# Two neighbouring rows of w_down on a partition: one layout of the expert weights against another

## The chip, the cores and the metric

The kernel runs on one core of a Trainium2 chip (trn2); the other cores are idle. The metric is the device time of one execution in microseconds, smaller is better; several executions give a median. Engine names are those of the profile: PE is TensorE (PEld its weight loads), DVE is VectorE, ACT ScalarE, POOL GpSimd, SP SyncE, whose queue issues nearly all DMAs. A line such as L188 is a line of the kernel before.

## The reference, cut to what matters

The program is one block of a streaming encoder on 256 frames of 1024 channels: a mixer (latent attention and a gated short convolution), then a mixture of 32 experts, of which each frame takes four. What the change touches is the second half:

```python
def expert_block(args):
    xb, e = args
    gu = xb @ w_gu[e] + b_gu[e]
    gate, up = gu[:, :D_EXPERT], gu[:, D_EXPERT:]
    gate = jnp.minimum(gate, SWIGLU_LIMIT)
    up = jnp.clip(up, -SWIGLU_LIMIT, SWIGLU_LIMIT)
    act = (up + 1.0) * (gate * jax.nn.sigmoid(gate * SWIGLU_ALPHA))
    return act @ w_down[e] + b_down[e]
```

All is float32. For one expert `w_gu[e]` is 1024 x 2048 (8 MB of 1024 x 1024 bytes each) and `w_down[e]` is 1024 x 1024 (4 MB). The sum over the 1024 channels of `act @ w_down[e]` may be taken in any order, so long as the activation's channel and the row of `w_down` that it multiplies belong together.

## The kernel before, in words

The mixer comes first (some 260 us), then a loop over the 32 experts. Each expert has at most 64 frames (`CAP`); more than that would be handled by `beyond()`, whose branch is not taken on these inputs.

**Weights.** The experts' weights stream through a ring of 22 slots of 8 KB a partition (`slot`, tag `wslot`). `todo` (L162 to L168) sets the order of the loads: the eight chunks of `w_gu` of expert e, then the four of `w_down` of expert e-1, and so on; the loads of a chunk are 1 MB each (`prefetch`, L171). A chunk of `w_gu` (L185) is 128 rows, one row of 8 KB on each partition. A chunk k of `w_down` (L188) is 256 rows; by the view `dn_v` (L159) partition p takes row 256k + p and row 256k + 128 + p, two pieces of 4 KB that lie 512 KB apart in memory. The last expert's `w_down` (L174 to L182) is loaded in another cut, first the columns 0 to 255 and 512 to 767, then the others, in pieces of 1 KB.

All these loads are issued by SP in the order of `todo`. The program hands out eight DMA semaphores in turn, so an issue waits until the DMA eight issues before it has landed; it also waits until the slot that it writes is free, which is PE's doing. The waits as the program has them, for the last whole expert but one on SP (DMAHW0 to DMAHW7 are the eight semaphores, PE the release of the slot):

```order
L188 DMA wslot<-in_w_down 128x2x1024 [waits DMAHW7_49,PE_49]
L188 DMA wslot<-in_w_down 128x2x1024 [waits DMAHW0_49,PE_49]
L188 DMA wslot<-in_w_down 128x2x1024 [waits DMAHW1_49,PE_49]
L188 DMA wslot<-in_w_down 128x2x1024 [waits DMAHW2_49,PE_49]
L185 DMA wslot<-in_w_gu 128x2048 [waits DMAHW3_49,PE_49]
L185 DMA wslot<-in_w_gu 128x2048 [waits DMAHW4_49,PE_49]
L185 DMA wslot<-in_w_gu 128x2048 [waits DMAHW5_49,PE_49]
L185 DMA wslot<-in_w_gu 128x2048 [waits DMAHW6_49,PE_49]
L185 DMA wslot<-in_w_gu 128x2048 [waits DMAHW7_49,PE_49]
L185 DMA wslot<-in_w_gu 128x2048 [waits DMAHW0_49,PE_49]
L185 DMA wslot<-in_w_gu 128x2048 [waits DMAHW1_49,PE_49]
L185 DMA wslot<-in_w_gu 128x2048 [waits DMAHW2_49,PE_49]
```

Counted back by eight in this cycle of twelve, the four `w_down` issues wait for the first four `w_gu` loads of the same cycle, the first four `w_gu` issues for the last four `w_gu` loads of the cycle before, and the last four `w_gu` issues for that cycle's `w_down`. The change leaves these waits as they are.

**Compute.** For an expert, `gate_up` multiplies its 64 gathered frames by the eight `w_gu` chunks into `pg` (L1014); the gate's half-columns 0 to 511 stand on PSUM partitions 0 to 63 and 512 to 1023 on 64 to 127. `act` (L1018) makes the activation `sgm`, 128 partitions by 512. `act_t` (L1028) turns it: four transposes on PE (L1031), each of 128 channels that are neighbours in `sgm`, and one copy by DVE to `aT` (L1033). `down` (L1043) takes the four `w_down` chunks, two row blocks a chunk, and multiplies each block with the columns of `aT` that hold its channels (`down_block`, L1040); DVE scales the result to `yp` (L1054). `scatter` (L1060) spreads two experts' `yp` to the 256 frames, in `acc`; every fourth expert `gather` (L982) picks the frames of the next four. The `down` of expert e-1 runs after the `gate_up` of expert e. For the last expert, e = 31, the `down` of e = 30 has the `act_t` of e = 31 in its middle (`late`), and then the last `down` goes in two column halves (L1220 ff.), each with its share of the scatter (L1242), of the squares (L1248) and of the output.

Of the kernel before, what the change touches and what calls it, by code (L numbers as in the profile page):

```python
# [16 lines left out]
P = 128  # L17
D = 1024
T = 256
NT = 2  # L20
NQ = 8
# [10 lines left out]
DE = 1024  # L32
# [19 lines left out]
def ap_of(a, offset, dims):  # L52
    return bass.AP(tensor=a.tensor, offset=a.offset + offset, ap=dims)
# [3 lines left out]
def block_kernel(ctx, tc, x, c, positions, w_ada, b_ada, norm_mix_g, w_in, q_norm_g, w_uq, kv_norm_g,  # L57
                 w_ukv, w_up_attn, conv_w, w_up_conv, w_o, norm_ffn_g, router_w, router_b, w_gu, b_gu,
                 w_down, b_down, norm_final_g, out, dbg=None):
    nc = tc.nc  # L60
    V, S, G, TE = nc.vector, nc.scalar, nc.gpsimd, nc.tensor
    load = nc.sync.dma_start
# [10 lines left out]
    def slot(shape, name="wslot", dtype=F32):  # L73
        t = slots.tile([P, 2048], dtype, name=name, tag="wslot")
        n = 1
        for s in shape:
            n *= s
        t = t[:, :n]
        if len(shape) == 2:
            t = t.rearrange("p (a b) -> p a b", b=shape[1])  # L80
        elif len(shape) == 3:
            t = t.rearrange("p (a b c) -> p a b c", b=shape[1], c=shape[2])
        return t
# [20 lines left out]
    ident = keep.tile([P, P], F32, name="ident")  # L104
# [51 lines left out]
            V.tensor_scalar(dst, ps, a_col[:, n, j:j + 1], sh_col[:, n, j:j + 1], op0=ALU.mult, op1=ALU.add)  # L156

    gu_v = w_gu.rearrange("o e (q p) f -> p (o e) q f", p=P)
    dn_v = w_down.rearrange("o e (k q p) d -> p (o e) k q d", q=2, p=P)  # L159


    todo = []  # L162
# [8 lines left out]
    def prefetch(n):  # L171
        while len(here) < n and todo:
            e, k = todo.pop(0)
            if e == NE - 1 and k >= NQ:  # L174

                w = slot([4, 2, 256])
                b = 4 * ((k - NQ) % 2)
                cols = ap_of(w_down, (e * DE + b * P) * D + 256 * ((k - NQ) // 2),
                             [[D, P], [P * D, 4], [512, 2], [1, 256]])
                for q in ([slice(0, 4)] if k % 2 == 0 else (slice(0, 2), slice(2, 4))):  # L180
                    for h in range(2):
                        load(w[:, q, h], cols[:, q, h])  # L182
            elif k < NQ:
                w = slot([2048])
                load(w, gu_v[:, e, k, :])  # L185
            else:
                w = slot([2, D])
                load(w, dn_v[:, e, k - NQ])  # L188
            here.append(w)

    with tc.tile_pool(name="front", bufs=1) as fr, \
            tc.tile_pool(name="tp", bufs=4, space=bass.MemoryType.PSUM) as tpp:

        def tpt():
            return tpp.tile([P, 512], F32, name="tp")
# [94 lines left out]
        for q2 in range(4):  # L290
            p = tpt().rearrange("p (q t) -> p q t", t=T)
# [103 lines left out]
        for half in range(2):  # L395
            for k in range(4):
                q = 4 * half + k
                S.activation(hT[0][:, q, :], xps[q // 2][:, q % 2, :], AF.Identity, bias=sh_col[:, 0, q:q + 1],
                             scale=a_col[:, 0, q:q + 1])
                q = 4 * half + (k + 2) % 4  # L400
# [329 lines left out]
        for h in range(2):  # L730
            p = tpt()
# [168 lines left out]
        p = tpt()  # L900
# [5 lines left out]
        p = tpt()  # L906
# [53 lines left out]
    def pmt():  # L960
        return pmi.tile([P, 512], F32, name="pm")
# [9 lines left out]
    def gather(rks, hs=None, oh=None):  # L971

        n = len(rks) * CAP
        c = slice(4 * CAP - n, 4 * CAP)
        oh = (onehot(rks) if oh is None else oh).rearrange("p i a b -> p i (a b)")
        hs = hs or hsel()
        for q2 in range(4):
            p = pmt()[:, :2 * n].rearrange("p (q c) -> p q c", c=n)
            for q in range(2):
                qs = slice((2 * q2 + q) * P, (2 * q2 + q + 1) * P)  # L980
                for i in range(NT):
                    TE.matmul(p[:, q, :], xs[:, i, qs], oh[:, i, :n], start=(i == 0), stop=(i == NT - 1))  # L982
            for q in range(2):
                affine(hs[q2 // 2][:, 2 * (q2 % 2) + q, c], p[:, q, :], 1, 2 * q2 + q, q2)
        return hs

    def placed(rks, ws):

        ow = mo.tile([P, NT, 2, CAP], F32, name="ow", bufs=1)
        for i in range(NT):  # L990
            for k in range(2):
                V.tensor_scalar(ow[:, i, k, :], iota2[:, 0, :], rks[k][:, i, :], ws[k][:, i, :],
                                op0=ALU.is_equal, op1=ALU.mult)
        return ow

    def spread(ow):

        p = pmt()
        for i in range(NT):
            TE.transpose(p[:, i * P:(i + 1) * P], ow[:, i].rearrange("p a b -> p (a b)"), ident)  # L1000
        s2 = mo.tile([P, T], F32, name="s2")
        S.activation(s2, p[:, :T], AF.Copy)  # L1002
        return s2
# [14 lines left out]
    def act(pg):  # L1018
        ga = mo.tile([P, 512], F32, name="ga", bufs=1)
        sgm = mo.tile([P, 512], F32, name="sgm")  # L1020
        V.tensor_scalar(ga, pg[:, 0, :], LIMIT, None, op0=ALU.min)  # L1021
        S.activation(sgm, ga, AF.Sigmoid, scale=ALPHA)  # L1022
        V.tensor_scalar(pg[:, 1, :], pg[:, 1, :], LIMIT, -LIMIT, op0=ALU.min, op1=ALU.max)
        V.tensor_mul(ga, ga, sgm)
        V.scalar_tensor_tensor(sgm, pg[:, 1, :], 1.0, ga, op0=ALU.add, op1=ALU.mult)
        return sgm

    def act_t(a):  # L1028
        p = pmt().rearrange("p (q c) -> p q c", c=P)
        for q in range(4):  # L1030
            TE.transpose(p[:, q, :], a[:, q * P:(q + 1) * P], ident)  # L1031
        aT = mo.tile([P, 4, P], F32, name="aT")
        V.tensor_copy(aT, p)  # L1033
        return aT
# [28 lines left out]
    def chunk(k):  # L1063
        prefetch(1)
        return here.pop(0)
# [8 lines left out]
    def beyond():  # L1074

        cur = keep.tile([P, 1], F32, name="cur")
        lane = keep.tile([P, NE], F32, name="lane")
        V.memset(cur, 0.0)
        G.iota(lane, pattern=[[1, NE]], base=0, channel_multiplier=0, allow_small_or_imprecise_dtypes=True)
        at = keep.tile([P, NE], F32, name="at")  # L1080
        pick = keep.tile([P, NE], F32, name="pick")
        we = keep.tile([P, NT, 1], F32, name="we")
        re = keep.tile([P, 5, NT, 1], F32, name="re")
        row = slot([2, 2, 512], "row")
        ring = [slot([2, D], "ring") for _ in range(4)]
        reg = nc.values_load(flag[0:1, 0:1], min_val=0, max_val=T)
        with tc.If(reg > CAP):
            with tc.For_i(0, NE, 1) as e:
                G.dma_start(row[0:1], b_gu[:, bass.ds(e, 1), :].rearrange("o a (n g f) -> (o a) n g f", n=2, f=512))
                gu_e = w_gu[:, bass.ds(e, 1)].rearrange("o a (q p) f -> p (o a q) f", p=P)  # L1090
                dn_e = w_down[:, bass.ds(e, 1)].rearrange("o a (k p) d -> p (o a k) d", p=P)

                def gu_in(q):
                    w = ring[q % 4].rearrange("p a b -> p (a b)")
                    G.dma_start(w, gu_e[:, q, :])
                    return w

                def dn_in(k):
                    G.dma_start(ring[k], dn_e[:, 2 * k:2 * k + 2, :])
                    return ring[k]  # L1100

                V.tensor_scalar(at, lane, cur, None, op0=ALU.is_equal)
                V.tensor_scalar(cur, cur, 1.0, None, op0=ALU.add)
                for i in range(NT):
                    V.scalar_tensor_tensor(pick, at, 1.0, rk[:, i, :], op0=ALU.mult, op1=ALU.mult,
                                           accum_out=re[:, 0, i, :])
                    V.scalar_tensor_tensor(pick, at, 1.0, wgt[:, i, :], op0=ALU.mult, op1=ALU.mult,
                                           accum_out=we[:, i, :])
                for b in range(1, 5):
                    V.tensor_scalar(re[:, b], re[:, 0], -float(b * CAP), None, op0=ALU.add)  # L1110
                rks = [re[:, b] for b in range(1, 5)]
                hb = gather(rks)

                def bias_row(n, o):
                    for g in range(2):
                        TE.matmul(o[64 * g:64 * g + 64, :], ones[0:1, :64], row[0:1, n, g, :], start=True,
                                  stop=False, skip_group_check=True)

                for b in range(3):
                    if b % 2 == 0:  # L1120
                        s2 = spread(placed(rks[b:b + 2], [we, we]))
                        yp = mo.tile([P, D], F32, name="yp", bufs=1)
                    a = act(gate_up(hb, CAP * b, bias_row, gu_in))
                    down(act_t(a), dn_in, yp, b % 2)
                    if b == 1:
                        scatter(s2, yp)
                scatter(s2, yp, CAP)
# [5 lines left out]
    for e in range(NE):  # L1133
# [24 lines left out]
        a = act(pg)  # L1158
# [33 lines left out]
        if e == 10:  # L1192
# [9 lines left out]
            p = pmt()  # L1202
# [4 lines left out]
            for h in range(2):  # L1207
                p = pmt()
# [6 lines left out]
        if e == 18:  # L1215
            gfin_b = mo.tile([P, D], F32, name="gfin_b", tag="gfin", bufs=1)
            G.dma_start(gfin_b[0:1, :], norm_final_g.rearrange("(o d) -> o d", o=1))
            for h in range(2):
                p = pmt()
# [7 lines left out]
    o = slot([NT, D], "o")  # L1227
    s2 = s2s.pop(NE // 2 - 1)
    aT = down(aT, chunk, yp, 0, a)
    for c in range(2):  # L1230
        cs = slice(256 * c, 256 * c + 256)
        py = pmt()[:, :256]
        for b in range(8):
            if b % 4 == 0:
                w = chunk(b)
# [56 lines left out]
```

## Time and profile before

| | us |
|---|---|
| median of 3 runs | 1198.37 (1194.8 to 1198.66) |
| the profiled execution | 1196.22 |
| its span, first to last instruction | 1194.5 |
| PE busy | 1075.9 |
| DVE busy | 387.0 |
| ACT busy | 152.5 |
| POOL busy | 101.5 |
| PE's granted clock, mean share | 0.958 |

The profile's busy times are times in which an instruction of the engine is under way. PE's matmuls overlap in its pipeline and wait there, so a busy PE is not a PE at its peak. DMA traffic is shown apart, as the mean busy share of the 16 DMA engines and as GB/s. The chain of waits, followed back from the last instruction, gives 25% of the span to DMA and 14% to PE, and stops some 490 us before the end.

### The profile page before, as it was taken

The numbers are of one execution on the slowest core, as the hardware profiler recorded it, in microseconds if no ns is written. First come the engines' busy times: TensorE is split into PE (matmuls) and PEld (weight loads), VectorE is DVE, ScalarE is ACT, GpSimd is POOL, SyncE is SP. The second block draws the span as 40 slices with busy tenths as digits, with TensorE's granted clock in tenths as the row PEclk, the third lists the DMA queues.
The fourth block names the chain that finished last, engine by engine and source line by source line (L and its number), as shares of the span: only waits on it lengthen the run. The fifth ranks groups of instructions, "written<-read, shape, count | busy, mean of one in ns | idle before, by whom it ended". The sixth has DMA issues, their size and how long they took to land. (4 is left out here: it accounts for less than half of the span.)

```text
span 1194.5 us, 12133 instructions
## 1 busy us (share of the span) xinstructions
PE 1075.9 (90%) x4867; PEld 487.4 (41%) x4867; DVE 387.0 (32%) x713; ACT 152.5 (13%) x262; POOL 101.5 (8%) x99
## 2 busy tenths in 40 slices
PE   5897897989999999999998869999988988898886
PEld 1895685754343343333332233334323322342223
DVE  3789789333221231122221111221212211212113
ACT  2634542212000010000000000010000000000001
POOL 0635125210000000000000000000000000000000
PEclk8899897979999999998999988999999999999999
DMA  9984686689999999999999999999999999999995
GB/s 375 342 305 157 240 344 271 249 359 394 416 417 418 416 417 416 417 418 416 416 417 417 414 418 416 416 417 417 417 418 416 417 417 417 417 416 417 418 416 204
DMA packets 94056, 457.71 MB, mean 383 GB/s; under 512 B 8519, under 2 KB 13688, under 8 KB 60204
## 3 DMA queue, kind: packets, MB, share of 16 engines
q1 hardware_dynamic: 92730, 456.62, 94.6%
q8 instruction: 40, 0.66, 0.2%
q10 hardware_dynamic: 1186, 0.14, 0.1%
q0 software_dynamic: 80, 0.14, 0.0%
q14 instruction: 20, 0.16, 0.0%
HBM read 455.81 MB, written 1.05 MB: 382 GB/s over the span
## 5 line engine op out<-in xcount | busy, mean ns | idle before, releaser
L1014 PE MATMUL pg<-wslot,hsel 128*64 128x512 f32 x2048 | 466.0, 604 | 30.8 <-DMA wslot<-in_w_gu 30.8
L1014 PEld LDWEIGHTS pg<-wslot,hsel 128*64 128x64 f32 x2048 | 140.0, 138 | 341.5 <-issue 247.9
L1040 PE MATMUL pm<-wslot,aT 128*64 128x512 f32 (+1 forms) x1056 | 230.9, 583 | 14.6 <-DMA wslot<-in_w_down 12.2
L1021 DVE TENSOR_SCALAR ga<-pg 128x512 f32<-128x512 f32 x32 | 22.1, 692 | 462.3 <-PE pg L1014 447.1
L1040 PEld LDWEIGHTS pm<-wslot,aT 128*64 128x64 f32 x1056 | 72.8, 137 | 167.9 <-issue 127.1
L1022 ACT ACTIVATE sgm<-ga 128x512 f32<-128x512 f32 x32 | 20.2, 630 | 696.0 <-DVE ga L1021 696.0
L1054 DVE TENSOR_TENSOR yp<-gfx,pm 64x512 f32<-64x512 f32 x62 | 42.5, 686 | 205.0 <-PE pm L1040 204.4
L1136 POOL CAST sel<-id 128x256 fp32r<-128x256 f32 x32 | 12.9, 403 | 816.7 <-PE pg L1139 816.7
L331 POOL TENSOR_TENSOR wlo<-wslot,whi 128x2048 fp32r<-128x2048 f32 (+2 forms) x14 | 71.2, 5101 | 100.4 <-ACT whi L329 72.0
L982 PE MATMUL pm<-oh,xs 128*128 128x256 f32 (+1 forms) x256 | 59.1, 390 | 6.3 <-DVE oh L968 4.9
L982 PEld LDWEIGHTS pm<-oh,xs 128*128 128x128 f32 x256 | 49.3, 199 | 19.4 <-issue 13.0
L1060 PE MATMUL mm<-yp,s 128*128 128x512 f32 x120 | 54.9, 600 | 0.8 <-DVE yp L1054 0.8
L426 DVE SCALAR_TENSOR_TENSOR ada_acc<-wslot,cact,ada_acc 128x1024 f32<-128x1024 f32 x28 | 49.5, 1769 | 0.7
L329 ACT ACTIVATE whi<-wslot 128x2048 fp32r<-128x2048 f32 (+3 forms) x26 | 46.6, 1840 | 20.6 <-DMA wslot<-in_w_in 11.4
L1060 PEld LDWEIGHTS mm<-yp,s 128*128 128x128 f32 x120 | 22.1, 190 | 30.0 <-issue 27.5
L331 DVE TENSOR_TENSOR wlo<-wslot,whi 128x2048 fp32r<-128x2048 f32 (+1 forms) x12 | 30.0, 2514 | 6.1 <-ACT whi L329 4.2
L1031 PE MATMUL pm<-ident,sgm 128*128 128x128 f32 x128 | 21.4, 291 | 10.7 <-ACT s L1002 8.2
L318 PE MATMUL mm<-hTh,wlo 128*128 128x256 f32 x96 | 28.1, 293 | 2.4 <-POOL wlo L331 2.4
L316 PE MATMUL mm<-hTh,whi 128*128 128x256 f32 x96 | 28.0, 292 | 0.0
L317 PE MATMUL mm<-hTl,whi 128*128 128x256 f32 x96 | 27.8, 290 | 0.0
L1139 PE MATMUL pg<-bg,sel 128*128 128x512 f32 x64 | 25.0, 473 | 1.3 <-DVE hsel L156 1.3
L156 DVE TENSOR_SCALAR hsel<-pm,a_col,sh_col 128x256 f32<-128x256 f32 (+1 forms) x32 | 15.6, 531 | 32.0 <-PE pm L982 21.5
(308 smaller groups left out, 827.5 us busy)
## 6 DMA issues: line engine op xcount, KB each, us to landing
wslot<-in_w_gu SPq DMA_DIRECT2D x256, 1024.0 KB
wslot<-in_w_down SPq DMA_DIRECT2D x124, 1024.0 KB
wslot<-in_w_ada SPq DMA_DIRECT2D x24, 1024.0 KB
wslot<-in_w_in SPq DMA_DIRECT2D x14, 1024.0 KB
wslot<-in_w_o SPq DMA_DIRECT2D x4, 1024.0 KB
wslot<-in_w_up_conv SPq DMA_DIRECT2D x2, 1024.0 KB
wslot<-in_w_up_attn SPq DMA_DIRECT2D x2, 1024.0 KB
wslot<-in_w_down SPq DMA_DIRECT2D x4, 512.0 KB
```

The lines of the kernel that those rows point to most:

```text
L316: TE.matmul(o, l[0], r[0], start=start, stop=False, skip_group_check=True)
L317: TE.matmul(o, l[0], r[1], start=False, stop=False, skip_group_check=True)
L318: TE.matmul(o, l[1], r[0], start=False, stop=stop, skip_group_check=True)
L329: S.activation(hi, raw, AF.Copy)
L331: eng.tensor_tensor(lo, raw, hi, op=ALU.subtract)
L426: V.scalar_tensor_tensor(a, w[:, j, :], cj, a, op0=ALU.mult, op1=ALU.add)
L982: TE.matmul(p[:, q, :], xs[:, i, qs], oh[:, i, :n], start=(i == 0), stop=(i == NT - 1))
L1014: TE.matmul(pg[64 * g:64 * g + 64, n, :], hs[k // 4][:, k % 4, c0:c0 + CAP], w[:, f0:f0 + 512], start=False, stop=(k == NQ - 1), skip_grou ...
L1040: TE.matmul(py[64 * h:64 * h + 64, :], aT[:, qa, 64 * g:64 * g + 64], w[:, h], start=(b == 0), stop=(b == 7), skip_group_check=True)
L1054: V.tensor_mul(yp[64 * k2:64 * k2 + 64, h * 512:(h + 1) * 512], gfx[hp, :], py[hp, :])
L1060: TE.matmul(acc[i][h], s2[:n, i * P:(i + 1) * P], yp[:n, h * 512:(h + 1) * 512], start=start, stop=False, skip_group_check=True)
L1139: TE.matmul(o, sel[:, 2 * n:2 * n + 2, :].rearrange("p g c -> p (g c)"), bg2[:, e // 16, :], start=True, stop=False, skip_group_check=True)
```

## The change

The view of `w_down` goes from `(k q p)` to `(k p q)`: partition p of chunk k now takes the rows 256k + 2p and 256k + 2p + 1, which are neighbours, 8 KB in one piece. So that the channels still meet their rows, transpose q of `act_t` reads every second channel of a stretch of 256: the even ones or the odd ones. The last expert's loads follow the same rule, cut into pairs of row blocks; the same rule stands in `beyond()`.

```diff
-    dn_v = w_down.rearrange("o e (k q p) d -> p (o e) k q d", q=2, p=P)
+    dn_v = w_down.rearrange("o e (k p q) d -> p (o e) k q d", q=2, p=P)
...
-                cols = ap_of(w_down, (e * DE + b * P) * D + 256 * ((k - NQ) // 2),
-                             [[D, P], [P * D, 4], [512, 2], [1, 256]])
                 for q in ([slice(0, 4)] if k % 2 == 0 else (slice(0, 2), slice(2, 4))):
-                    for h in range(2):
-                        load(w[:, q, h], cols[:, q, h])
+                    for c in range(q.start, q.stop, 2):
+                        cols = ap_of(w_down, (e * DE + (b + c) * P) * D + 256 * ((k - NQ) // 2),
+                                     [[2 * D, P], [D, 2], [512, 2], [1, 256]])
+                        for h in range(2):
+                            load(w[:, c:c + 2, h], cols[:, :, h])
...
-            TE.transpose(p[:, q, :], a[:, q * P:(q + 1) * P], ident)
+            TE.transpose(p[:, q, :], a[:, 256 * (q // 2) + q % 2:256 * (q // 2) + 256:2], ident)
```

On SP, at the end of the program, the rows before are these (shape of the destination, then how many in a row):

```order
L185 DMA wslot<-in_w_gu 128x2048 x8
L188 DMA wslot<-in_w_down 128x2x1024 x4
L182 DMA wslot<-in_w_down 128x4x256 x2
L182 DMA wslot<-in_w_down 128x2x256 x4
L182 DMA wslot<-in_w_down 128x4x256 x2
L182 DMA wslot<-in_w_down 128x2x256 x4
L1268 DMA out<-o 128x512 x4
```

And now, in the changed kernel's line numbers:

```order
L187 DMA wslot<-in_w_gu 128x2048 x8
L190 DMA wslot<-in_w_down 128x2048 x4
L184 DMA wslot<-in_w_down 128x2x256 x16
L1271 DMA out<-o 128x512 x4
L1291 UNCONDITIONAL_BRANCH
```

Every one of the 124 whole chunks of `w_down` has the shape of a `w_gu` chunk now, and the last expert's 12 loads are 16, all of 256 KB. Nothing else has another place on any engine.

## Rows read from the trace of the kernel before

**Rows 1.** The page, part 2: GB/s in 40 slices of 29.86 us; DMA packets by size.
```profile
GB/s 375 342 305 157 240 344 271 249 359 394 416 417 418 416 417 416 417 418 416 416 417 417 414 418 416 416 417 417 417 418 416 417 417 417 417 416 417 418 416 204
DMA packets 94056, 457.71 MB, mean 383 GB/s; under 512 B 8519, under 2 KB 13688, under 8 KB 60204
```
**Rows 2.** Stretches: length, busy us of PE, PEld, DVE, ACT, POOL; PEclk, DMA share, GB/s.
```profile
250.00:300.00 50.00, 48.24 (x226) 22.06 (x227) 14.31 (x40) 7.97 (x15) 2.07 (x5) 0.92 0.92 370
300.00:350.00 50.00, 49.53 (x224) 20.71 (x222) 11.96 (x28) 3.68 (x7) 0.69 (x2) 1.00 1.02 416
350.00:500.00 150.00, 146.93 (x660) 54.53 (x658) 33.05 (x64) 6.34 (x12) 2.42 (x6) 1.00 1.02 417
740.00:817.00 77.00, 76.18 (x330) 29.19 (x328) 16.70 (x34) 5.51 (x10) 0.81 (x2) 0.96 1.02 417
817.00:938.00 121.00, 110.61 (x484) 39.21 (x480) 25.29 (x49) 5.33 (x10) 1.61 (x4) 1.00 1.02 417
```
**Rows 3.** Groups by line, 817 to 938 us: PE's matmuls, idle time before them, releaser.
```profile
L1014 PE MATMUL pg<-wslot,hsel 128*64 128x512 f32 x256 | 58.8, 599 | 6.9 <-DMA wslot<-in_w_gu 6.9
L1040 PE MATMUL pm<-wslot,aT 128*64 128x512 f32 x146 | 33.0, 596 | 2.4 <-DMA wslot<-in_w_down 2.4
```
**Rows 4.** SP's own waits, 820 to 1150 us: us in total, times, longest.
```profile
SPq L185 <- DMA wslot<-in_w_down: 91.7, 44, 2.2
SPq L188 <- DMA wslot<-in_w_gu: 89.7, 43, 3.3
SPq L185 <- PE pg L1014: 44.2, 26, 4.5
```
**Rows 5.** SP's issues in order of time, 817 to 945 us: start, length.
```profile
820.05 18.00 SPq L185 DMA_DIRECT2D wslot<-in_w_gu  x8
840.20 9.26 SPq L188 DMA_DIRECT2D wslot<-in_w_down  x4
850.14 18.00 SPq L185 DMA_DIRECT2D wslot<-in_w_gu  x8
870.30 9.17 SPq L188 DMA_DIRECT2D wslot<-in_w_down  x4
880.24 18.00 SPq L185 DMA_DIRECT2D wslot<-in_w_gu  x8
900.41 9.26 SPq L188 DMA_DIRECT2D wslot<-in_w_down  x4
910.35 17.97 SPq L185 DMA_DIRECT2D wslot<-in_w_gu  x8
```
**Rows 6.** SP's issues of the first experts, 225 to 330 us.
```profile
240.18 1.98 SPq L188 DMA_DIRECT2D wslot<-in_w_down  x4
...
270.74 12.00 SPq L188 DMA_DIRECT2D wslot<-in_w_down  x4
...
297.82 7.63 SPq L188 DMA_DIRECT2D wslot<-in_w_down  x4
```
**Rows 7.** Timeline from 1155 us to the end, SP and PE; in brackets idle time before.
```profile
1152.68 22.83 SPq L182 DMA_DIRECT2D wslot<-in_w_down  x12
...
1160.17 1.94 PE L1014 MATMUL pg<-wslot,hsel 128*64 128x512 f32 x8 [0.58 <-DMA wslot<-in_w_gu]
...
1169.26 0.66 PE L1031 MATMUL pm<-ident,sgm 128*128 128x128 f32 x4
...
1173.20 3.55 PEld L1040 LDWEIGHTS pm<-wslot,aT 128*64 128x64 f32 x31 [0.16 <-DMA wslot<-in_w_down]
```
**Rows 8.** Stretches of the last 25 us, columns as in rows 2.
```profile
1175.00:1180.00 5.00, 4.49 (x32) 2.84 (x28) 1.17 (x4) 1.54 (x7) 0.00 (x0) 1.00 0.96 314
1180.00:1185.00 5.00, 4.48 (x37) 2.88 (x34) 1.60 (x5) 0.66 (x4) 0.00 (x0) 1.00 0.08 28
```
**Rows 9.** The tile sgm: ns of one (min/median/max), first and last start, form.
```profile
L1031 PEld LDWEIGHTS pm<-ident,sgm x128: 137/141/230, 275.8 to 1169.5; 128*128 128x128 f32 x128
```

More of the change, by code (lines that the diff above doesn't have):

```diff
@@ L1090, in beyond @@
                 gu_e = w_gu[:, bass.ds(e, 1)].rearrange("o a (q p) f -> p (o a q) f", p=P)
-                dn_e = w_down[:, bass.ds(e, 1)].rearrange("o a (k p) d -> p (o a k) d", p=P)
+                dn_e = w_down[:, bass.ds(e, 1)].rearrange("o a (k p q) d -> p (o a k) q d", q=2, p=P)
                 def gu_in(q):
@@ L1098, in dn_in @@
                 def dn_in(k):
-                    G.dma_start(ring[k], dn_e[:, 2 * k:2 * k + 2, :])
+                    G.dma_start(ring[k], dn_e[:, k])
                     return ring[k]
```

## The prediction

> **What bounds the kernel now.** I read the page's slices first, then a table of stretches, then SP's issues one by one. The slices show the traffic [rows 1]: uneven for the first third, while the mixer runs, and then from the eleventh slice to the last but one 414 to 418 GB/s, flat. The stretches say the same with PE beside it [rows 2]: from 300 us on the 16 DMA engines are busy without a gap (share 1.02) at 416 to 417 GB/s, whatever PE does. PE is busy 99% of 740 to 817 us and 91% of 817 to 938 us, and the traffic is the same in both, so DMA sets the pace in both, and PE's higher share in the first is a backlog that it works off. Where the backlog is gone, PE's idle time before the expert matmuls is ended by the weights: 6.9 us before `gate_up` and 2.4 us before `down` in the 121 us of four experts [rows 3]. So from about 300 us to the landing of the last `w_gu` chunk the time is bytes over rate. What follows that landing is PE's: the first matmuls on that chunk start at 1160.17 us [rows 7], and 34.3 us remain to the end of the span.
>
> **The price of a w_down load.** SP's issues measure it. Each waits for the landing of the DMA eight before it: `w_gu` issues wait for `w_down` 44 times in 820 to 1150 us, four in each of 11 experts, and `w_down` issues for `w_gu` 43 times [rows 4]. So the start of an issue is the landing of the load eight before, and the distance of two issues is the time that the DMA engines gave to the loads between. From the first `w_down` issue of a cycle to the next first `w_gu` issue four `w_gu` loads land: 850.14 - 840.20 = 9.94 us, and 9.94 again twice [rows 5], which is 2.485 us for one, 422 GB/s (1.0486 MB each). From the first `w_gu` issue to the first `w_down` issue four `w_gu` and four `w_down` land: 20.15, 20.16 and 20.17 us [rows 5]. Less 9.94 that leaves 10.22 us for four `w_down` loads, 2.555 us for one, 410 GB/s. A load of the same megabyte in two pieces of 4 KB a partition is 0.07 us dearer than one in pieces of 8 KB, and the four of an expert 0.28 us.
>
> After the change such a load has the form of a `w_gu` load in every respect: the same 1 MB of consecutive memory, 8 KB of it on each partition, the same slot. So I price it with the `w_gu` row, not with a rule: 0.28 us less for each expert.
>
> [...]
>
> **The sum.** The `w_down` loads of experts 0 to 29 land before the last `w_gu` chunk of expert 31. Those of experts 0 and 1 are issued at 240.18 and 270.74 us [rows 6], when the engines were not yet full (370 GB/s, share 0.92 [rows 2]); a cheaper load buys between nothing and 0.28 us each there; I take nothing, since the share was below 1 and something other than the engines held the queue. From expert 2, issued at 297.82 us [rows 6], on it counts fully: 28 x 0.28 = 7.8 us. The last chunk of `w_gu` lands 7.8 us earlier, and with it everything that PE does after.
>
> **Edits that I cost at nothing.** (a) The transposes. Four weight loads of `sgm` an expert read with a gap of one element; no row shows such a read. The nearest is the same load without gaps, 141 ns [rows 9]; below that it can't go, since it reads as many elements. The dearest of its 128 instances, 230 ns, is the bound above: 4 x 0.09 = 0.4 us an expert. For 31 experts that lies under PE's wait for weights, (6.9 + 2.4) / 4 = 2.3 us an expert [rows 3]; for the last the transposes stand on the path (0.66 us at 1169.26 [rows 7]), so the bounds on the end are 0 and 0.4 us, and I take 0 by the nearest row. [...]
>
> (b) The last expert's `w_down` is 16 loads of 256 KB in place of 12 of 256 or 512 KB: as many pieces of 1 KB, four issues more. What hides them is the queue: eight loads are under way, 2 MB, 6.7 us at the 314 GB/s of this stretch [rows 8], and SP needs 22.83 us for twelve issues only because they wait for landings [rows 7]. PE waits 0.16 us for the first of these loads [rows 7], and the traffic is over soon after 1180 us (28 GB/s from there [rows 8]). If the cover went, say at 5% less than 314 GB/s, 4.2 MB would take 0.7 us longer; against that the last whole expert's `w_down` ends 0.28 us sooner. Bounds: 0.3 us less to 0.7 us more; I take 0.
>
> (c) PE's demand. If PE now became late, slots would hold SP. That already happens without harm: 26 issues waited 44.2 us for `gate_up` in 820 to 1150 us [rows 4], at full traffic, since seven other loads are still queued. The cycle goes from 30.1 to 29.8 us, and PE keeps 2.0 of its 2.3 us of slack.
>
> The sum stands against the profiled execution: 1196.22 - 7.8 = 1188.4 us. That execution lay 2.15 us under the median of the three runs; as the result will be a median too, the predicted time is 1198.37 - 7.8 = 1190.6 us.
>
> **The rivals.**
>
> *Part of the 0.07 us is not the pieces.* What the issues measure might be in part a cost of changing from one kind of load to the other, or of this place in the cycle, and stay. If half stays, the gain is 28 x 0.14 = 3.9 us: 1194.5 us. Against it: the four loads form a block, and two changes in a cycle of twelve leave little to share. Chance 0.08. [...]
>
> *PE or the slots take the gain.* If PE set the pace wherever it looks full, in 300 to 500 us and 740 to 817 us [rows 2], then (200 + 77) / 30.1 = 9.2 experts give nothing: 7.8 - 2.6 = 5.2 us, 1193.2 us; with as much again between 500 and 740 us, 3.0 us and 1195.4 us. Against it speaks the traffic, 417 GB/s there as elsewhere. Chance 0.06.
>
> *The pieces stay 4 KB.* Source and destination are each one stretch of memory now, but a DMA might still be cut at the row. Then nothing changes: 1198.4 us. Against it: the program's load now reads as 128x2048, as `w_gu`'s does, and the profile's packets fit loads of that shape not being cut (60204 of 94056 are under 8 KB, so some 33,850 are 8 KB or more; the 256 chunks of `w_gu` and 8 of the same form from `w_ada` make 264 x 128 = 33,792 [rows 1]). Chance 0.03.
>
> *Slower: the gapped read.* If the weight load pays for every element it skips, the place is `act_t`, on PE, 32 times. It decides from the point where four loads cost more than the 2.3 us of slack [rows 3], 0.58 us each on top of 0.141, five times today's. At eight times (1.13 us a load, 3.95 us more an expert) each of 31 experts would lose 3.95 - 2.3 = 1.65 us and the last 3.95: 51 + 4 = 55 us, less 7.8: 1246 us. Nothing in the trace speaks for it but that it is unseen. Chance 0.03.
>
> **How the numbers follow.** The forecast has 0.80, the rivals 0.08, 0.06, 0.03 and 0.03. What a measurement can tell from no change is about 0.3%, 3.6 us, so "faster" means under 1194.8 us. The forecast, half of the first rival and half of the second, 0.87, less 0.03 for medians of three runs that spread over 3.9 us: faster 0.84. Slower is the last rival and a little of that spread, 0.04. The rest, 0.12, is no change. The range: below, the lowest run shown, 1194.8, with 31 experts counted, 8.7 us: 1186. Above, the second rival's worse case, 1195.4, rounded to 1195.5; the first lies inside. It leaves out the third rival and the last, and the tails.
>
> **What would show it.** Right: the issues of a cycle of twelve 29.8 us apart, with no difference between the four `w_down` landings and four of `w_gu` (9.94 and 9.94); slices at 420 to 421 GB/s; some 15,900 fewer packets (124 x 256 of 4 KB become 124 x 128 of 8 KB); the last `w_gu` matmuls at 1152 to 1153 us; four transposes still 0.66 us; 34 us after that. Wrong: the packets' number unchanged (third rival); `w_down` still at 10.1 to 10.2 us for four (first); traffic below 419 GB/s with idle time of PE gone (second); the weight loads of `sgm` above 0.7 us (fourth). A tail longer than 35 us would mean that (a) or (b) costs something after all.

## The result and the profile after

| | before | after |
|---|---|---|
| median, us | 1197.38 (1194.8 to 1198.66, 4 runs) | 1188.65 (1188.09 to 1189.88, 4 runs) |
| ratio | | 0.9931, 95% interval 0.9917 to 0.9944 |
| the profiled execution, us | 1196.22 | 1188.36 |
| its span, us | 1194.5 | 1186.7 |

The kernel is 8.7 us faster by the medians, 7.86 us by the two profiled executions; the forecast was a gain of 7.8 us and 1190.6 us. The runs that came with the result moved the median of before from 1198.37 to 1197.38 us, so that half of the 1.95 us between forecast and measurement is the reference's own.

The page of the kernel after, part 2, as [rows 1]:

```profile
GB/s 373 339 305 157 231 368 240 269 335 399 420 422 421 422 420 421 421 421 421 421 421 421 421 420 420 421 421 421 421 422 421 421 421 421 421 421 421 422 420 204
DMA packets 78248, 457.71 MB, mean 386 GB/s; under 512 B 8583, under 2 KB 13752, under 8 KB 28524
```

From the eleventh slice on 414 to 418 GB/s have become 420 to 422, and 15,808 packets are gone (forecast 15,900). What is missing from 124 x 128 = 15,872 are 64 more packets under 512 B, beside four more loads for the last expert.

Two stretches of the kernel after, columns as in [rows 2]:

```profile
740.00:817.00 77.00, 76.18 (x342) 30.04 (x340) 18.77 (x37) 5.51 (x10) 1.21 (x3) 1.00 1.01 421
811.00:931.00 120.00, 109.56 (x474) 38.73 (x472) 24.63 (x48) 5.33 (x10) 1.61 (x4) 1.00 1.01 421
```

PE is as full in the first as it was [rows 2], and the traffic is 421 GB/s in both. SP's issues in order of time, 800 to 945 us (start, length), as [rows 5]:

```profile
815.76 17.71 SPq L187 DMA_DIRECT2D wslot<-in_w_gu  x8
835.64 7.78 SPq L190 DMA_DIRECT2D wslot<-in_w_down  x4
845.58 17.71 SPq L187 DMA_DIRECT2D wslot<-in_w_gu  x8
```

A cycle is 845.58 - 815.76 = 29.82 us. From the first `w_gu` issue to the first `w_down` issue it takes 19.88 us, from there to the next `w_gu` issue 9.94. The four `w_gu` landings are still 9.94, so four `w_down` are 19.88 - 9.94 = 9.94: the difference of 0.28 us an expert is gone to the last digit.

PE's groups by line, 811 to 931 us, as [rows 3]:

```profile
L1016 PE MATMUL pg<-wslot,hsel 128*64 128x512 f32 x256 | 58.9, 600 | 7.2 <-DMA wslot<-in_w_gu 7.1
L1043 PE MATMUL pm<-wslot,aT 128*64 128x512 f32 x142 | 32.1, 596 | 2.2 <-DMA wslot<-in_w_down 2.2
```

PE still waits for weights, 9.4 us in four experts (9.3 before). The tile `sgm`, as [rows 9], and PE at the end, 1150 us on, as [rows 7]:

```profile
L1034 PEld LDWEIGHTS pm<-ident,sgm x128: 194/209/231, 276.9 to 1162.2; 128*128 128x128 f32 x128
```
```profile
1152.76 1.94 PE L1016 MATMUL pg<-wslot,hsel 128*64 128x512 f32 x8 [0.55 <-DMA wslot<-in_w_gu]
...
1161.85 0.74 PE L1034 MATMUL pm<-ident,sgm 128*128 128x128 f32 x4
1162.52 7.11 PE L1043 MATMUL pm<-wslot,aT 128*64 128x512 f32 x48
```

The gapped weight load takes 209 ns where the plain one took 141, and the last group of four 0.74 us where it took 0.66. The last `w_gu` matmuls start at 1152.76 us, 7.41 us earlier than in [rows 7], and the span ends 33.94 us behind them (34.33 before).

**Where the 7.8 us of the span came from.** The six `w_gu` issues just ahead of the first `w_down` load begin 0.99 us later than before (225.91 against 224.92 us): that is the mixer, which the change doesn't touch. At expert 5's first `w_gu` issue the lag is 0.36 us (335.54, 335.18), at expert 31's it is a lead of 7.10 (1115.51, 1122.61). So the experts before gave 0.63 us and the 26 cycles between 7.46, 0.287 each. From there to the last `w_gu` matmuls, while another expert's `w_down` lands, the lead grows by 0.31 to 7.41, and the tail adds 0.39. The rows of those issues:

```profile
224.92 12.47 SPq L185 DMA_DIRECT2D wslot<-in_w_gu  x6
335.18 18.05 SPq L185 DMA_DIRECT2D wslot<-in_w_gu  x8
1122.61 17.97 SPq L185 DMA_DIRECT2D wslot<-in_w_gu  x8
```
```profile
225.91 12.47 SPq L187 DMA_DIRECT2D wslot<-in_w_gu  x6
335.54 18.31 SPq L187 DMA_DIRECT2D wslot<-in_w_gu  x8
1115.51 17.71 SPq L187 DMA_DIRECT2D wslot<-in_w_gu  x8
```

In the profiled executions of six kernels of this study whose programs are the same up to that point (these two, `near4k`, `plain_t`, `pe2` and `pe6`), the first of those six issues starts between 223.86 and 225.91 us. The kernel after is the latest of them, so its 0.99 us is read as the spread of single executions.

### The profile page after: what moved, and what is told of

It reads as the page before. It is cut to its first block, busy times and chain, and to the rows that moved or that the text cites. A ratio compares the mean times of both kernels' runs of the same rounds, so it can differ in the third digit from the quotient of the medians.

```text
span 1186.7 us, 12137 instructions
## 1 busy us (share of the span) xinstructions
PE 1074.6 (91%) x4867; PEld 491.1 (41%) x4867; DVE 386.3 (33%) x713; ACT 152.5 (13%) x262; POOL 101.5 (9%) x99
## 5 line engine op out<-in xcount | busy, mean ns | idle before, releaser
L1034 PE MATMUL pm<-ident,sgm 128*128 128x128 f32 x128 | 24.1, 312 | 10.7 <-ACT s L1004 8.2
L1034 PEld LDWEIGHTS pm<-ident,sgm 128*128 128x128 f32 x128 | 18.0, 208 | 26.7 <-issue 12.2
L156 DVE TENSOR_SCALAR hsel<-pm,a_col,sh_col 128x256 f32<-128x256 f32 (+1 forms) x32 | 15.6, 531 | 32.7 <-PE pm L984 21.5
```

The lines of the kernel that those rows point to most:

```text
L1034: TE.transpose(p[:, q, :], a[:, 256 * (q // 2) + q % 2:256 * (q // 2) + 256:2], ident)
```

## The experiments

The theory: a load's price is its bytes plus a fixed price for each piece of consecutive memory, and DMA sets the pace throughout, so 124 loads with half the pieces end the program sooner by what the loads save. Rivals: the 512 KB between a partition's two pieces cost, not their number; the change from one kind of load to the other costs; PE or the slots decide; the gapped read costs.

**1. `stream`: loads alone.** The program is nothing but SP's loads, 32 in a row of each kind, into a ring of ten buffers, with one DVE copy of a column per load.

```diff
+    far = w_down.rearrange("o e (k q p) d -> p (o e) k q d", q=2, p=P)
+    near = w_down.rearrange("o e (m p q c) d -> p (o e) m c q d", q=2, c=2, p=P)
+    pair = w_down.rearrange("o e (k p q) d -> p (o e) k (q d)", q=2, p=P)
+    four = w_down.rearrange("o e (m p q) d -> p (o e) m (q d)", q=4, p=P)
+    half = w_down.rearrange("o e (k q p) (h d) -> p (o e) k h q d", q=4, h=2, p=P)
```

> All computation is left out: only SP streams expert weights from memory into a ring, in eight stretches of 32 loads, and the output is zeros. The stretches: 8 KB pieces; 4 KB pieces 512 KB apart; 4 KB pieces 8 KB apart; 8 KB again; 16 KB pieces (2 MB loads); 2 KB pieces 512 KB apart; w_gu as it is; 4 KB pieces 512 KB apart again. Theory (the size of a piece sets the price): 2.485 us a MB for 8 KB and for w_gu, 2.555 for both kinds of 4 KB; if each piece has a fixed price, 0.07 us being that of 8 more pieces a DMA engine, 2.695 for 2 KB and 2.45 for 16 KB. Rival (the jump of 512 KB between a partition's two pieces costs it): 4 KB pieces 8 KB apart go at 2.485. Rival (a change between two kinds of load in the cycle costs it): all stretches of 4 KB go at 2.485 too, since nothing alternates within a stretch.

Stretches inside each row of 32 (length, busy us of DVE and POOL, PEclk, DMA share, GB/s), in the order 8 KB pieces, 4 KB 512 KB apart, 4 KB 8 KB apart, 8 KB, 16 KB, 2 KB, `w_gu`, 4 KB 512 KB apart:

```profile
10.00:60.00 50.00, 3.08 (x20) 0.00 (x0) 1.00 1.01 423
80.00:145.00 65.00, 3.84 (x25) 0.00 (x0) 1.00 1.02 409
165.00:228.00 63.00, 3.84 (x25) 0.00 (x0) 1.00 1.03 409
240.00:305.00 65.00, 3.84 (x25) 0.00 (x0) 1.00 1.02 421
340.00:430.00 90.00, 2.77 (x18) 0.00 (x0) 1.00 1.01 428
492.00:555.00 63.00, 3.54 (x23) 0.00 (x0) 1.00 1.05 387
575.00:630.00 55.00, 3.38 (x22) 0.00 (x0) 1.00 1.01 422
650.00:715.00 65.00, 3.85 (x25) 0.00 (x0) 1.00 1.03 410
```

From issue to the eighth issue behind it, by eight, a 1 MB load takes 2.485 us in 8 KB pieces, 2.56 in 4 KB pieces, near or far, 2.711 in 2 KB pieces, and 2.447 for each MB in 16 KB pieces. The rates in the rows say the same: 1.0486 MB at 423, 409, 387 and 428 GB/s are 2.48, 2.56, 2.71 and 2.45 us. The first two are the prices that the forecast read out of the kernel's own cycle, 2.485 and 2.555. The steps go with the number of pieces: halving 8 KB adds 128 pieces a load, 8 for each of the 16 engines if they share evenly, and 0.075 us, halving 4 KB adds 16 for each and 0.151 us, joining two 8 KB removes 4 a MB and 0.038 us: 9.4, 9.4 and 9.5 ns a piece. Distance in memory (8 or 512 KB, 409 GB/s both), and the array (421 to 423 GB/s both), cost nothing here. Nor can the price be SP's handing out of the pieces alone: an issue takes 0.33 us in the median with 8 KB pieces, and 0.33 us also where a single issue of 16 KB pieces stands by itself (`wide_all` at 419.75 us, `wide_l7` at 902.43 and 997.05), and the step between these two still has the same price a piece.

**2. `near4k`: 4 KB pieces again, but neighbours.** Partition p takes the rows 4p, 4p + 2 of 512 (and 4p + 1, 4p + 3), so that its two pieces lie 8 KB apart, and the transposes read every fourth channel.

```diff
-    dn_v = w_down.rearrange("o e (k p q) d -> p (o e) k q d", q=2, p=P)
+    dn_v = w_down.rearrange("o e (m p q c) d -> p (o e) m c q d", q=2, c=2, p=P)
...
-            TE.transpose(p[:, q, :], a[:, 256 * (q // 2) + q % 2:256 * (q // 2) + 256:2], ident)
+            TE.transpose(p[:, q, :], a[:, q // 2 + 2 * (q % 2):512:4], ident)
```

> The changed kernel, but partition p takes of 512 rows the rows 4p and 4p+2 in one chunk and 4p+1 and 4p+3 in the other: pieces of 4 KB again, 8 KB apart and not 512 KB; the transposes read every fourth channel. Theory (size of the piece): four w_down loads 10.2 us again, cycle 30.1 us, time that of the kernel before, 1196 to 1198 us. Rival (the jump of 512 KB): cycle 29.82 us, 1188 to 1189 us. The weight loads of sgm, 209 ns with a gap of one element, should rise above that with a gap of three; PE has the slack, so the time shows nothing of it but 0.1 to 0.4 us at the last expert.

1198.21 us against 1197.16, ratio 1.0012 (1.0002 to 1.0021). SP's issues:

```profile
822.92 18.00 SPq L187 DMA_DIRECT2D wslot<-in_w_gu  x8
843.08 9.24 SPq L190 DMA_DIRECT2D wslot<-in_w_down  x4
853.02 18.00 SPq L187 DMA_DIRECT2D wslot<-in_w_gu  x8
```

The cycle is 30.10 us again, with 20.16 from `w_gu` to `w_down` and 9.94 back. All of the change's other parts are in this kernel (gapped reads, 16 loads at the end), only the size of the pieces is undone, and the gain is gone whole. It is even 0.1% slower than before, at the edge of the interval: its profiled span is 2.4 us longer, and 2.7 us more passed between the issues at 225 us and expert 5's first `w_gu` issue (112.96 us against 110.26). Why is open. Its tile `sgm` tells something besides:

```profile
L1034 PEld LDWEIGHTS pm<-ident,sgm x128: 195/210/226, 276.2 to 1172.4; 128*128 128x128 f32 x128
```

A gap of three elements costs what a gap of one costs, 210 ns against 209; the expected rise isn't there.

**3. `gu4k`: the change's opposite on `w_gu`.** Its chunks become two half rows of 4 KB on a partition, as `w_down`'s were; `w_down` stays as changed, and the matmuls of `gate_up` take each half row with its rows' channels.

```diff
-    gu_v = w_gu.rearrange("o e (q p) f -> p (o e) q f", p=P)
+    gu_v = w_gu.rearrange("o e (m r p) (n f) -> p (o e) m n r f", r=2, n=2, p=P)
...
-                load(w, gu_v[:, e, k, :])
+                load(w, gu_v[:, e, k // 2, k % 2])
```

> The changed kernel with the opposite done to w_gu: a chunk holds the gate's or the up's 1024 columns of two row blocks, 4 KB pieces 1 MB apart, the same matmuls in another order. Theory (size of the piece): eight loads at 2.555 instead of 2.485 us, cycle 29.82 + 0.56 = 30.4 us, 30 experts x 0.56 = 17 us slower than the changed kernel, about 1205 us. Rival (a change between kinds in the cycle costs it): alternation is back, but w_gu itself should stay at 9.94 us for four and the time grow by no more than 9 us.

1205.7 us, ratio 1.0078 (1.0061 to 1.0095). The cycle:

```profile
824.54 21.18 SPq L187 DMA_DIRECT2D wslot<-in_w_gu  x8
845.82 7.31 SPq L190 DMA_DIRECT2D wslot<-in_w_down  x4
854.95 22.03 SPq L187 DMA_DIRECT2D wslot<-in_w_gu  x8
```

30.41 us: 8 loads at 2.56 and 4 at 2.485 make 30.42. Against the kernel after that is 0.59 us an expert and 17 us in all: twice as many loads, twice the change, with its sign turned.

**4. `plain_t`: the change without the gaps.** The transposes read neighbours as before, so that channels meet other rows of `w_down`.

> The changed kernel with the transposes reading neighbouring channels as before: the channels meet other rows of w_down. Theory (the gapped weight load costs 209 against 141 ns, hidden behind DMA but for the last expert): weight loads of sgm back to 141 ns, group of four at the last expert 0.66 us, time within 0.3 us of the changed kernel, 1188.3 us. Rival (the gapped read delays PE and with it slots): 1186.5 us or less, 31 x 0.07 us earlier.

1187.83 us, ratio 0.9927 (0.991 to 0.9943), against 0.9931 (0.9917 to 0.9944) for the change: no difference that these runs can tell. The weight loads of `sgm`, and the last group:

```profile
L1034 PEld LDWEIGHTS pm<-ident,sgm x128: 137/141/143, 275.9 to 1160.8; 128*128 128x128 f32 x128
```
```profile
1160.48 0.66 PE L1034 MATMUL pm<-ident,sgm 128*128 128x128 f32 x4
```

The gap costs 68 ns a load, but a group of four is only 0.74 - 0.66 = 0.08 us longer on PE. The loads, 194 ns or more each, lie partly over one another and over the matmuls: the last four are under way for 0.55 us together in the kernel after and for 0.42 us before, and the first of them starts at 1161.84 us in the kernel after, 0.07 us before the matmuls ahead of it end (1158.26 + 3.65). For all experts but the last the difference is hidden: from expert 5's first `w_gu` issue to expert 31's it takes 780.45 us here and 779.97 in the kernel after.

**5. `pe2` and `pe6`: PE's slack.** The four transposes are made three times, and seven times.

```diff
-        for q in range(4):
+        for q in list(range(4)) * 3:
```

> The changed kernel with every group of four transposes done three times. With seven times, 28 transposes took 3.63 us without a gap, 0.121 us each past the first, so two more groups are 1.0 us an expert. Theory (2.35 us of slack an expert): hidden but for the last expert, 1.0 us slower than the changed kernel, 1189.6 us. Rival (PE sets the pace in the stretches where it is busy throughout): 10 to 20 us slower.

1188.49 us, ratio 0.9932 (0.9915 to 0.9948): nothing lost in the loop, where a cycle still takes 29.82 us (`w_down` issues from 863.47 and from 893.29 us). The 1.0 us that the expectation gave to the last expert is in the trace, where the span ends 34.93 us behind the last `w_gu` matmuls' start in place of 33.94; in the median it is lost in the spread. PE's idle time before `gate_up`, 811 to 931 us, has paid for the eight more transposes an expert:

```profile
L1016 PE MATMUL pg<-wslot,hsel 128*64 128x512 f32 x256 | 56.8, 596 | 2.0 <-DMA wslot<-in_w_gu 2.0
```

> The changed kernel with every group of four transposes of the activation done seven times, the same values again. One more group costs PE about 0.67 us (from the first transpose to the next matmul at the last expert), six 4.0 us an expert. Theory (DMA sets the pace, PE has 2.3 us of slack an expert): (4.0 - 2.35) x 29 + 4 = 52 us slower than the changed kernel, about 1240 us. Rival (PE sets the pace already): 32 x 4.0 = 128 us slower, about 1317 us. Rival (PE has far more slack): 4 us slower, the last expert alone.

1217.68 us, one run: slower, but 22 us less so than was expected. The expectation priced the 24 transposes more at 4.0 us an expert; a group of 28 takes 3.63 us in the trace, so that they cost 2.9 (3.63 less 0.74), 0.6 us above the slack and not 1.7. With that, 31 x 0.6 + 2.9 = 21.5 us would make 1210, and the trace shows where more is lost. In two pairs of slices the traffic falls, to 378 and 392 GB/s (577 to 638 us) and to 358 and 402 GB/s (729 to 791 us); against 421 GB/s that is 11 us of traffic. In the first pair PE's expert matmuls wait for no load (0.0 us idle before them, 570 to 640 us), and PE is busy 62.47 of the 63 us from 577 to 640 us while the DMA engines' share is 0.95; in the second PE is busy 52.75 of 60 us (730 to 790 us, share 0.94), and what held the traffic there is not shown. Expert 31's first `w_gu` issue comes 9.1 us later than in the kernel after (1124.64 us, 1115.51), and from it to the end it takes 91.4 us in place of 71.2: at the end PE works off a backlog (its last 64 `gate_up` matmuls run from 1167.19 us for 13.95 us without a wait for a load). So here PE does set the pace in places, which the forecast's second rival supposed of the kernel before. Elsewhere the traffic keeps its rate though PE is full, as in 811 to 931 us:

```profile
811.00:931.00 120.00, 118.65 (x572) 52.32 (x568) 24.59 (x48) 6.53 (x12) 1.61 (x4) 1.00 1.01 421
```

The two together place the point from which a dearer read would show: 1.0 us an expert (1.71 us for a group of 12 less 0.74) is free, 2.9 us is not. The forecast's slack of 2.3 us lies between.

**6. `stream2`: is there a price for changing kinds?** Loads alone again: five cycles of 8 `w_gu` and 4 loads of 4 KB pieces, then 8 of 4 KB and 4 of 8 KB, then rows of one kind.

> All computation is left out, as in the first stream. Five cycles of eight w_gu loads and four w_down loads of 4 KB pieces (512 KB apart); five cycles of eight loads of 4 KB pieces and four of 8 KB; 32 loads of 4 KB pieces in a row; 64 loads of half the size, one 4 KB piece a partition; 12 loads of twice the size, four 4 KB pieces a partition. In the first stream a MB in 4 KB pieces took 2.63 us in a row of 32, in the kernel 2.555 among loads of 8 KB. Theory (a long row of 4 KB pieces is dearer, because SP can't hand out its eight loads at once): first cycle 30.1 us as in the kernel, second 30.4 us, the row 2.63 us. Rival (the kernel's other traffic makes the difference): both kinds of cycle at 2.63 us for a 4 KB load, 30.4 and 31.0 us. If handing out is the cause, the loads of half the size go at 2.6 us a MB or better and those of twice the size at 2.63.

SP's issues in the first and the second part:

```profile
15.68 18.03 SPq L111 DMA_DIRECT2D wide<-in_w_gu  x8
35.87 8.66 SPq L86 DMA_DIRECT2D wide<-in_w_down  x4
45.81 18.04 SPq L111 DMA_DIRECT2D wide<-in_w_gu  x8
...
167.45 21.49 SPq L86 DMA_DIRECT2D wide<-in_w_down  x8
189.03 7.10 SPq L92 DMA_DIRECT2D wide<-in_w_down  x4
197.87 21.98 SPq L86 DMA_DIRECT2D wide<-in_w_down  x8
```

30.13 and 30.42 us a cycle: 8 x 2.485 + 4 x 2.56 = 30.12, and 8 x 2.56 + 4 x 2.485 = 30.42. The prices add, with nothing for the changes. The rows of one kind, all in 4 KB pieces, go at 410 GB/s as loads of 1 MB (300 to 360 us), at 410 as loads of half that size (390 to 455 us) and at 409 as loads of twice that size (465 to 525 us), 2.56 us a MB each: the size of a load makes no difference. The 2.63 us that the expectation speaks of, and its theory of a dearer long row, rest on a misreading of `stream`: 57.80 us had been divided by the 22 issues in them, though the issues of 4 KB loads, 0.37 to 4.72 us long, come in groups and not evenly.

**7. Larger pieces: `wide_d`, `wide_all`, `wide_l7`, `wide_l11`, `wide_l15`.** If a piece costs 9.4 ns, 16 KB pieces should give 12 x 0.038 = 0.46 us an expert more. `w_down` with four neighbouring rows on a partition, and `w_gu` with two (the gather of the frames then reads every second channel), go in 2 MB loads into a ring of ten buffers, which takes the place of the slots once the mixer no longer needs those. The five differ in the expert behind which that happens: in `wide_d` after expert 1 and for `w_down` alone (the 1 MB loads of `w_gu` fill halves of a buffer), in `wide_all` after expert 1 and for `w_gu` from expert 4 on, in the others after expert 7, 11 and 15 for both, with the last `w_gu` load split in two.

```diff
+    dn_v = w_down.rearrange("o e (m p r) d -> p (o e) m (r d)", r=4, p=P)
+    gu_2 = w_gu.rearrange("o e (m p r) f -> p (o e) m (r f)", r=2, p=P)
...
+                t = wide[0].tile([P, 4096], F32, name="wwide", tag="wide")
+                whole = gu_2[:, e, k // 2] if k < NQ else dn_v[:, e, (k - NQ) // 2]
...
+                    load(t, whole)
...
+        if e == 7:
+            assert not here
+            early.close()
+            wide.append(ctx.enter_context(tc.tile_pool(name="wide", bufs=10, side="right", reuse_waits="tile")))
```

> A version that goes further: after expert 1 the ring has 10 slots of 16 KB, and two chunks of w_down come as one load of 2 MB, four neighbouring rows (16 KB) on a partition; w_gu comes as before, 1 MB into each half of a slot. By the first stream 16 KB pieces take 2.447 us a MB against 2.485. Theory (a fixed price of a piece, hidden by nothing): 28 experts x 4 x 0.038 = 4.3 us less than the changed kernel, about 1184 us. Rival (the coarser ring lets the DMA engines run dry or PE wait for whole loads): no faster than the changed kernel, 1188 us or more.

> The same, and from expert 4 on w_gu also comes in loads of 2 MB, two neighbouring rows (16 KB) on a partition, with the gathered frames' channels reordered to match. Theory: 28 experts x 12 x 0.038 = 12.8 us less than the changed kernel, about 1176 us, less some 2 us because the last w_gu load now brings two chunks at once: 1176 to 1178 us. Rival (coarser ring): no faster than 1184 us.

1211.52 us, ratio 1.0124 (1.0107 to 1.0141), and 1204.41 us, 1.0071 (1.0053 to 1.0088): slower than before, though the stream is faster. `wide_all`'s slices:

```profile
GB/s 374 333 333 161 236 316 301 249 32 362 422 429 427 426 426 426 427 427 427 427 428 426 427 427 423 426 427 427 427 427 427 427 427 427 427 427 427 427 422 181
```

427 GB/s where the kernel after has 421, but a hole of one slice, 30 us at 32 GB/s, where the change-over falls: (1 - 32 / 427) x 30 = 28 us of traffic at the full rate, 21 us of it beyond what the kernel after misses in that slice, where it has 335 GB/s. A 2 MB buffer must wait until both slots under it are read; that most of them hold weights just then that PE hasn't come to is argued from the order of the program, not shown.

> The version with 16 KB pieces, the ring changed over after expert 7 instead of expert 1 (where the first 2 MB slots had to wait for two small ones each and the DMA engines stood still for some 26 us), and the last two w_gu chunks as two loads. Theory: 24 experts x 8 + 25 x 4 = 292 MB at 0.038 us less, 11 us less than the changed kernel: 1177 to 1179 us if the change-over costs nothing, and the cycle of an expert 29.4 us. Rival (PE still has a backlog at expert 7, and the change-over leaves the engines idle again): a hole of 5 to 25 us in the traffic near 450 us, 1183 to 1203 us.

> The same with the change-over after expert 11. Theory: 20 experts x 8 + 21 x 4 = 244 MB at 0.038 us less, 9.3 us: 1179 to 1181 us, 2 us behind the one after expert 7. Rival (the backlog): a smaller hole than after expert 7, so faster than that one.

1185.28 us, ratio 0.9904 (0.9887 to 0.992), and 1190.71 us, 0.9959 (0.9937 to 0.998): neither reaches its expected time, and the later change-over is not the better one. The hole is smaller than in `wide_all`, not gone: one slice at 320 GB/s in `wide_l7`, one at 280 in `wide_l11`. SP's issues at the two, `wide_l7` first:

```profile
394.41 17.79 SPq L211 DMA_DIRECT2D wslot<-in_w_gu  x8
414.36 26.53 SPq L201 DMA_DIRECT2D wwide<-in_w_down  x2
440.94 2.82 SPq L201 DMA_DIRECT2D wwide<-in_w_gu  x4
```
```profile
513.42 17.78 SPq L211 DMA_DIRECT2D wslot<-in_w_gu  x8
556.66 0.80 SPq L201 DMA_DIRECT2D wwide<-in_w_down  x2
```

In `wide_l7` the second of the 2 MB loads, in `wide_l11` the first, is held for some 26 us, and those behind it with it. By the order in which PE reads the slots, the change-over after expert 15 should find the ones it needs first already read:

> As wide_l7 (16 KB pieces in a ring of ten 2 MB buffers), with the change-over after expert 15 in place of 7. If the hole in the traffic at the change-over (wide_l7: one slice at 320 GB/s; wide_l11: two at 280) comes from wide buffers that must wait for two old slots each, in an order of addresses that the first 16 KB loads go through: by the ages of the old slots at this point the order is a good one, no slice falls below 410 GB/s there, and the 16 experts behind it are each some 0.4 us cheaper (29.4 us a cycle against 29.82), as in wide_l7: 1188.7 - 16 x 0.4 = 1182 us. Rival: the hole belongs to any change-over, some 3 to 5 us, as in wide_l7 and wide_l11: then 1185 to 1188 us, with a slice at 320 GB/s or less near 630 us.

1183.58 us (1182.39 to 1184.49), ratio 0.9884 (0.9867 to 0.99). (`wide_l11` has one slice at 280 GB/s, not the two of the expectation.) The slices:

```profile
GB/s 374 327 301 154 241 366 239 270 336 396 420 420 420 420 419 420 419 419 420 419 420 419 423 427 426 426 427 427 426 426 429 427 426 427 427 427 427 427 423 190
```

No hole at all; behind the change-over most cycles take 29.4 us:

```profile
975.22 15.04 SPq L201 DMA_DIRECT2D wwide<-in_w_gu  x4
...
1004.64 16.54 SPq L201 DMA_DIRECT2D wwide<-in_w_gu  x4
```

It beats both kernels, 5 us under the kernel after. The expected 1182 us were missed by 1.6: ahead of the change-over the traffic is 419 to 420 GB/s and not 421, where this kernel's 8 KB pieces of `w_down` lie 16 KB apart and its slots are 21. Which of the two it is was not tried. `wide_l15` and `wide_l7` ran on different chips, and their intervals overlap, so that their order is shown by the holes, not by the ratios.

## Why the prediction was right

**The bound.** That DMA sets the pace wherever it runs at its full rate, also where PE looks full, is confirmed twice: 421 GB/s in 740 to 817 us with PE 99% busy, and `pe2`, which takes 1.0 us an expert out of PE's slack and loses nothing in the loop.

**The price.** 2.555 against 2.485 us a load, read from the distance of SP's issues, is what loads alone cost (2.56 and 2.485), and the priced row, `w_gu`'s, was the right one: `w_down` landed in 9.94 us afterwards, for four.

**The sum.** 28 x 0.28 = 7.8 us stands against 7.86 in the profiled executions and 8.7 in the medians (6.7 to 9.9 by the ratio's interval). The agreement to a tenth is partly luck: the stream gave 7.46 + 0.31 + 0.63 = 8.4 us, of which the loads of 28 experts by the measured cycle are 7.8, and the tail 0.39, while the mixer of that execution took 0.99 back. The 7.46 us of the 26 cycles are solid: from expert 5's first `w_gu` issue to expert 31's it takes 787.43 us before and 787.20 in `near4k`, with 4 KB pieces, 779.97 after and 780.45 in `plain_t`, with 8 KB pieces. The 0.63 us ahead of them are not shown to be the change's: from the issues at 225 us to expert 5's first `w_gu` issue it takes 110.26 us before and 109.63 after, but 112.96 in `near4k` and 108.66 in `plain_t`. So what experts 0 and 1 gave, taken at nothing, stays open.

**(a) The transposes** were taken at 141 ns, by the nearest row; they take 209, near the other bound, 230. The path felt only the last group, 0.08 us of the 0.4 allowed, because the loads overlap (0.55 us under way for the last four, 0.42 before). This is the one term whose choice was wrong, and it cost nothing because the cover named for it, 2.3 us an expert, held. With three elements between two that are read the load takes 210 ns (`near4k`), with one 209, with none 141 (`plain_t`).

**(b) The last expert's 16 loads** cost nothing: the tail is 33.94 us where it was 34.33. That is 0.1 us below the bounds of 0.3 less to 0.7 more. Of the 0.39 us, 0.16 lie ahead of the first `out` issue (28.45 us behind the last `w_gu` matmuls' start, 28.61 before), where PE's wait for the first of these loads, 0.16 us [rows 7], is gone. The other 0.23 lie behind that issue (5.49 us, 5.72 before), which the change doesn't touch. The forecast's reason for less, a last whole expert whose `w_down` ends 0.28 us sooner, is not what shows: `near4k`, with 4 KB pieces, has a tail of 33.91 us.

**(c) PE's demand.** The conclusion held, the reading behind it did not. The 44.2 us that SP waited for `gate_up` [rows 4] were taken for slots held by PE. The waits of SP in the kernel after, 820 to 1140 us:

```profile
SPq L187 <- DMA wslot<-in_w_down: 92.0, 44, 2.2
...
SPq L187 <- DMA wslot<-in_w_gu: 88.4, 42, 2.6
SPq L187 <- PE pg L1016: 1.2, 4, 0.4
```

They are gone although PE is no less busy (109.56 of 120 us in 811 to 931 us; before, 110.61 of 121 in 817 to 938 us), and in `near4k` they are back (40.9 us, 24 times, in 820 to 1150 us). What goes with 4 KB pieces is the length of SP's issues. Of the `w_gu` issues, before (820 to 1150 us) and after (820 to 1140 us), ns of one as min/median/max:

```profile
L185 SPq DMA_DIRECT2D wslot<-in_w_gu x88: 327/328/4628, 820.1 to 1140.3; - x88
```
```profile
L187 SPq DMA_DIRECT2D wslot<-in_w_gu x86: 327/328/328, 820.7 to 1132.9; - x86
```

PE isn't needed for that: `stream2` has no PE work, and there a `w_gu` issue among loads of 4 KB pieces takes up to 4.3 us too.

```profile
L111 SPq DMA_DIRECT2D wide<-in_w_gu x40: 327/364/4312, 0.7 to 124.5; - x40
```

Before, the first `w_gu` issue behind four loads of 4 KB pieces takes 3.97 to 4.63 us in each of the 11 cycles, those after it come late, and the row that ends some of their waits is then PE's. That the 44.2 us are nothing but this shadow is the likeliest reading; no run shows it directly. The traffic shows nothing of it, 417 GB/s in 817 to 938 us: eight loads of 2.5 us are under way.

**The rivals.** A part that stays (0.08): `stream2` gives the changes between kinds no price (30.13 us a cycle, 30.12 by the prices of single loads), and the kernel after shows the whole 0.28 us an expert. PE or the slots (0.06): `pe2`. Pieces that stay 4 KB (0.03): the packets' number, 15,808 fewer. The gapped read (0.03): dearer indeed, by half and not eight times (209 ns, 141); `pe6` shows where it would have begun to matter.

The measured 1188.65 us lies in the range of 1186.0 to 1195.5.

## What to carry to other kernels

Where the traffic is flat while DMA sets the pace (414 to 418 GB/s before), price a load by what the same queue's issues show of it. Here the four prices of `stream` come to some 2.41 us for the bytes of a MB (an estimate worked out from them) plus some 9.4 ns for each consecutive piece that a DMA engine takes (eight of 8 KB in a MB, by even shares), so that 4 KB pieces cost 2.8% (in the kernel) to 3.0% (alone) more than 8 KB ones and 16 KB ones 1.5% less, with 8 or 512 KB between them in memory. The reordering that longer pieces ask of the other operand may well cost something on PE (68 ns a weight load here); ask how much slack covers it, and what of it stands behind the last load. When buffers change size in mid-stream, the price is the hole at the change-over, 28 us of traffic in `wide_all` and none in `wide_l15`. That it goes by which of the old buffers have been read by then was foretold for `wide_l15` and came true there; no trace shows the buffers themselves.

## What the runs showed that was not expected

- The price of a piece is linear from 2 KB to 16 KB (2.711, 2.56, 2.485, 2.447 us a MB): no size in this range is the one from which it stops to matter, there is only less to gain.
- A float32 weight load of 128 x 128 with gaps takes 209 ns where 141 is the plain one's, and a gap of three costs no more than a gap of one (210).
- With loads in 4 KB pieces SP's own issues take 2.3 us in the median and up to 4.7 (`stream`; the median is 0.33 with 8 KB), while the DMA engines stay busy throughout (share 1.02 to 1.03); a wait that the profile puts down to an engine may be the shadow of that.
